# TensorE in written order through the prompt's MLP, with lasting score rows, tanh in PSUM and pair sums moved behind the MLP

## The chip, the core and the metric

The kernel runs on one core of a Trainium2 chip. The metric is device time of one execution in microseconds (us). Engines are named as in the profile: PE (TensorE, matrix products), DVE (VectorE), ACT (ScalarE), POOL (GpSimd) and SP (SyncE, which issues the DMAs). Each engine works through its own queue in a fixed order and waits on semaphores; In this kernel POOL is given operands in SBUF alone.

## The reference

One encoder layer is run on a prompt of 512 rows and, with the same weights, on a sample of 1024 rows, 1024 columns wide, all in float32.

```python
h = _rmsnorm(x, norm_attn_g[l])
z = h @ w_in[l]                         # q | k | v | ca | cb
a_out = _window_attn(q, k, v, bias, band, attn_sink[l])
c = ca * jax.nn.sigmoid(cb)
c = _dwconv(c, conv_dw_w[l], conv_dw_b[l])                     # 31 taps
c = jax.nn.silu(_layernorm(c, conv_ln_g[l], conv_ln_b[l]))
x = x + jnp.concatenate([a_out, c], axis=-1) @ w_out[l]
h = _rmsnorm(x, norm_ffn_g[l])
u = _dwconv(h @ w_up[l], ffn_dw_w[l], ffn_dw_b[l])             # 3 taps
x = x + (jax.nn.silu(u[..., :D_FF]) * u[..., D_FF:]) @ w_down[l]
return _rmsnorm(x, norm_final_g)

# in _window_attn: 8 heads of 64, 2 key heads, blocks of 128 queries against 3 blocks of keys
sc = einsum(qb, kb) * HEAD_DIM ** -0.5 + bias                  # masked to |q-k| <= 128
m = max(max(sc), sink)
p = exp(sc - m)
denom = sum(p) + exp(sink - m)
o = einsum(p / denom, vb)
```

## The kernel before

**Numbers.** A float32 product is made of three products of split operands: each operand is written as a high part (`hi`, type fp32r, a cast by ACT) and the low rest (`lo`, a subtraction), and hi x hi, hi x lo and lo x hi are added in PSUM. Weights are split by `split` (lines 142 and 143: the cast on ACT, the subtraction on POOL), activations where they leave PSUM.

**Buffers.** SBUF is cut into slots by size: 15 of 4096 bytes (`q`), 4 for padded conv rows (`c`), 61 of 2048 bytes (`h`), and small ones. A tile takes the free slot that has been free longest. PSUM has 8 banks: three `a`, two `u`, two `b`, one `c`; the table `use` says which job may take which.

**Stages.** (1) The prompt's 14 chunks of the input projection. (2) The same 14 chunks for the two halves of the sample (`step(i, 1)` and `step(i, 2)`), and beside them, as a side job, the prompt's attention, its conv norms, its output projection (`out_half`) and the transposes of its normalised rows for the MLP (`make_h2`, by `transposed`, line 208). (3) The prompt's MLP: 22 steps `ffn_step(k)`, each with two up projections of 24 products (`proj`, lines 249, 250 and 252), three taps (lines 766 and 762) and a `gate`; beside them, the sample's attention, from step `U0` on. (4) The sample's output projection. (5) The sample's MLP up, in a form with seven block products in place of eight, and then the down projection of the prompt and the sample together, for which sums of blocks of the prompt's gates are wanted (`gb`).

**Side jobs.** A side job is a generator. `proj` calls `tick()` after each six products and once more behind a step; a tick adds `rate` to an account and moves the side job by one `yield` for each whole unit in it. The 31-tap convolutions on DVE (line 292, one operation per tap, the accumulator in PSUM) are paced by the same tick, with the credits `conv` (the prompt's) and `late` (the sample's).

**Attention.** For a unit u (one block of 128 queries and one key head, four heads in it), `scores(u)` makes four score products (line 500), adds bias and finds the row's negated maximum in one DVE operation (line 503), takes Exp on ACT with the row's sum (line 512) and of the sink apart (line 516), adds the two (517), takes the reciprocal (518) and scales the four heads (522 on ACT, 524 on DVE or POOL, by the strings `SCB` for the prompt and `SCD` for the sample). `values(u)` turns the probabilities (four transposes by PE, line 545), splits what it gets into hi (ACT, 547) and lo (DVE, 548), and multiplies with the values (559 with hi, 560 with lo). Unit u+1 has its scores in front of unit u's values.

**What sets the order.** Up to the sample's MLP no order is written by hand: the framework's planner puts all instructions of all engines in order by a simulated timeline. From the sample's MLP on, PE stands in written order (`by_hand`, line 1146).

**The gate.** For gate column j of the prompt, ACT writes tanh into an SBUF tile; DVE multiplies (line 790), DVE or POOL multiplies with the value part (791). Of each pair of gates (j even and odd, called e and t), four differences and sums of halves are made at once (801, 805 and 807 on DVE, 803 on POOL), and seven tiles are stored to DRAM as `gb`.

## Time and profile before

| | |
|---|---|
| median of 3 runs | 1585.31 us (1583.26 to 1587.23) |
| profiled execution | 1580.89 us, its span 1579.1 us |
| mean granted TensorE clock in it | 0.983 |
| busy share of the span | PE 96%, DVE 77%, ACT 51%, POOL 44% |
| DMA | 219.97 MB, mean 139 GB/s |

The page lists the busy time of each engine, the span in 40 slices, the DMA queues, the costliest groups of instructions and what ended the idle time before them. A row of a group reads: line, engine, operation, output and inputs by name, shape, count, then busy time, mean duration in ns, and idle time before with its releaser. A row of the timeline reads: start, duration, engine, line, operation, and in brackets the idle time before it. A matmul's duration is longer than the distance to the next start, since matmuls overlap.

### The profile page before, as it was taken

To read this page: it belongs to the slowest core of one execution; us is meant where nothing else is said; L and a number is where in the kernel's file an instruction comes from. 1 tells how busy PE (TensorE), PEld (TensorE's weight loads), DVE (VectorE), ACT (ScalarE), POOL (GpSimd) and SP (SyncE) were. 2 spreads that over 40 slices of the span, in tenths; PEclk is the share of its full clock that TensorE was granted. 3 is DMA by queue.
4 is the path that set the end of the run, shared out by engine and by line. 5 is a ranking of instruction groups with operands and counts; after the bars stand their busy time and mean duration, and the time that the engine had idled before them with its cause. 6 is when DMAs were issued, how large, how long until landed. Compare 5 with 4: busy or idle time off the path is not lost. (4 is left out here: it accounts for less than half of the span.)

```text
span 1579.1 us, 20219 instructions
## 1 busy us (share of the span) xinstructions
PE 1519.8 (96%) x6843; PEld 1237.4 (78%) x6843; DVE 1211.3 (77%) x1661; ACT 805.3 (51%) x1476; POOL 687.1 (44%) x525
## 2 busy tenths in 40 slices
PE   8999998997998998999999999999999999999997
PEld 6778786886887787878887888888888788888886
DVE  7999865765989999775686787788786945668883
ACT  4635655336676676742455444444544633343354
POOL 6642443235575586751133455555555000003355
PEclk9999998997999999999999999999999999999999
DMA  7583255356443443856221333333332582346644
GB/s 233 155 209 90 81 127 136 108 155 161 147 141 106 137 137 104 240 189 201 94 76 53 109 104 100 100 107 101 100 107 73 191 303 77 121 155 219 216 151 160
DMA packets 222157, 219.97 MB, mean 139 GB/s; under 512 B 12532, under 2 KB 162876, under 8 KB 221925
## 3 DMA queue, kind: packets, MB, share of 16 engines
q1 hardware_dynamic: 222053, 218.67, 44.0%
q8 instruction: 54, 0.88, 0.2%
q14 instruction: 50, 0.41, 0.1%
HBM read 158.97 MB, written 60.70 MB: 139 GB/s over the span
## 5 line engine op out<-in xcount | busy, mean ns | idle before, releaser
L143 POOL TENSOR_TENSOR q<-q,q 128x1024 fp32r<-128x1024 f32 x72 | 176.5, 2456 | 94.4 <-ACT q L142 88.3
L866 DVE TENSOR_TENSOR h<-h,h 128x512 fp32r<-128x512 f32 (+2 forms) x202 | 156.0, 804 | 65.4 <-ACT h L870 25.1
L866 POOL TENSOR_TENSOR q<-q,q 128x512 fp32r<-128x512 f32 x82 | 113.6, 1397 | 160.0 <-ACT q L976 154.5
L1318 PE MATMUL w<-h,h 128*128 128x512 f32 x462 | 181.4, 393 | 0.5 <-DVE q L1108 0.5
L1320 PE MATMUL w<-h,h 128*128 128x512 f32 x462 | 181.7, 393 | 0.0
L1319 PE MATMUL w<-h,h 128*128 128x512 f32 x462 | 181.5, 393 | 0.0
L249 PE MATMUL u<-h,q 128*128 128x512 f32 x400 | 165.2, 414 | 10.7 <-DVE h L762 7.9
L250 PE MATMUL u<-h,q 128*128 128x512 f32 x400 | 162.7, 407 | 0.0
L252 PE MATMUL u<-h,q 128*128 128x512 f32 x384 | 155.0, 404 | 1.2 <-POOL q L143 1.2
L990 PE MATMUL w<-h,q 128*128 128x512 f32 x372 | 147.1, 396 | 1.8 <-ACT h L1070 0.9
L992 PE MATMUL w<-h,q 128*128 128x512 f32 x372 | 145.8, 392 | 0.6 <-POOL q L866 0.6
L292 DVE SCALAR_TENSOR_TENSOR c<-c,cvw,c 128x512 f32<-128x512 f32 x184 | 137.6, 748 | 2.1
L991 PE MATMUL w<-h,q 128*128 128x512 f32 x350 | 137.0, 391 | 0.0
L863 POOL TENSOR_TENSOR q<-q,q 128x1024 f32<-128x1024 f32 x12 | 33.2, 2774 | 236.0 <-DVE q L863 219.6
L870 ACT CAST h<-h 128x512 fp32r<-128x512 f32 x120 | 72.0, 619 | 93.7 <-DVE h L866 41.7
L249 PE MATMUL b<-h,q 128*128 128x512 f32 x256 | 102.7, 401 | 2.5 <-DVE d L322 1.6
L1318 PEld LDWEIGHTS w<-h,h 128*128 128x128 f32 x462 | 86.9, 188 | 20.5 <-ACT h L870 0.9
L249 PEld LDWEIGHTS u<-h,q 128*128 128x128 f32 x400 | 78.3, 196 | 31.1 <-DVE h L762 4.2
L142 ACT CAST q<-q 128x1024 fp32r<-128x1024 f32 x72 | 75.1, 1046 | 53.7 <-DMA q<-in_w_in 16.7
L1319 PEld LDWEIGHTS w<-h,h 128*128 128x128 f32 x462 | 86.8, 188 | 19.7
L1320 PEld LDWEIGHTS w<-h,h 128*128 128x128 f32 x462 | 86.8, 188 | 19.5
L252 PE MATMUL b<-h,q 128*128 128x512 f32 x256 | 101.8, 398 | 0.0
(427 smaller groups left out, 3889.8 us busy)
## 6 DMA issues: line engine op xcount, KB each, us to landing
q<-in_w_up SPq DMA_DIRECT2D x88, 512.0 KB
ga<-q SPq DMA_DIRECT2D x64, 256.0 KB
h<-ga SPq DMA_DIRECT2D x57, 256.0 KB
q<-in_w_in SPq DMA_DIRECT2D x28, 512.0 KB
h<-in_w_down SPq DMA_DIRECT2D x52, 256.0 KB
gb<-h SPq DMA_DIRECT2D x77, 128.0 KB
h<-gb SPq DMA_DIRECT2D x35, 256.0 KB
q<-in_x_sample SPq DMA_DIRECT2D x15, 512.0 KB
```

Of the source, the lines that this page charges most:

```text
L143: (nc.vector if dve else nc.gpsimd).tensor_tensor(lo[:], raw[:], hi[:].bitcast(F32), op=ALU.subtract)
L249: nc.tensor.matmul(out, whi[:, kc, :], hi[:], start=(kc == 0), stop=False)
L250: nc.tensor.matmul(out, whi[:, kc, :], lo[:], start=False, stop=False)
L252: nc.tensor.matmul(out, wlo[:, kc, :], hi[:], start=False, stop=(kc == KC - 1))
L292: nc.vector.scalar_tensor_tensor(acc[:], src(t), w(t), acc[:], op0=ALU.mult, op1=ALU.add)
L866: (eng or nc.vector).tensor_tensor(out, a, b, op=ALU.subtract)
L990: nc.tensor.matmul(out, whi[:, s], hi[:], start=(start and c == 0), stop=False, **go)
L991: nc.tensor.matmul(out, whi[:, s], lo[:], start=False, stop=False, **go)
L992: nc.tensor.matmul(out, wlo[:, s], hi[:], start=False, stop=(stop and c == 3), **go)
L1318: nc.tensor.matmul(out, sh[:, c], th[:], start=(p == 0), stop=False)
L1319: nc.tensor.matmul(out, sh[:, c], tl[:], start=False, stop=False)
L1320: nc.tensor.matmul(out, sl[:, c], th[:], start=False, stop=(p == NPAIR - 1))
```

## The change

The change does these things in the stretch from the sample's projections to the end of the prompt's MLP, and a little behind it:

- PE stands in written order there (`manual_schedule` around stages 2 and 3); the other engines are still put in order by the planner.
- For each head there is a lasting row of scores in SBUF (`score_rows`, two heads in a tile of 4096 bytes, four tiles). Its column 0 holds the negated sink, written by DVE once per attention (`sink_columns`). Exp reads columns 0 to nk and writes a fresh tile, so that its row sum has the sink in it. The Exp of the sink and the add go.
- `gate` writes tanh into a PSUM bank of kind `b`, and stores the whole gate (`gt`). The sums of pairs become side jobs (`pair_sums`) that run behind the MLP, wholly on POOL, on gates that are loaded again. The down projection reads the plain blocks out of `gt`.
- One of four heads of the sample is scaled on ACT in place of DVE (`SCD`).
- The sample's keys and values are loaded ahead of the end of the convs (`load_kv`), and the first up weights in the last chunk of the projections. The sample's attention begins one MLP step later (`U0`), and the rates of the side jobs differ.

```diff
-RA, RB, RBO, RD, RN, RE = 1.2, 0.8, 2.5, 0.78, 0.95, 0.9
+RA, RB, RBO, RD, RN, RE = 1.2, 0.8, 2.5, 0.8, 0.95, 1.4
-CL, CLO, CD = 0.7, 0.7, 0.6
+CL, CLO, CD = 0.6, 1.0, 0.6
-SCB, SCD = "aapa", "vaap"
+SCB, SCD = "aapa", "aaap"
-U0 = 1
+U0 = 2
...
+    def sink_columns():
+        for h in range(0, NH, 2):
+            t = sb.tile([2, NT])
+            for n in range(2):
+                nc.vector.tensor_copy(t[:, n, 0:1], nsink[:, h + n:h + n + 1])
+            score_rows.append(t)
...
-                out=p[:, :nk], in0=sc[:, :nk], in1=bias[h][:, off:off + nk], scale=-1.0,
+                out=row_of(h)[:, 1:1 + nk], in0=sc[:, :nk], in1=bias[h][:, off:off + nk], scale=-1.0,
...
-            nc.scalar.activation(pr[j][:, :nk], pr[j][:, :nk], AF.Exp, scale=-1.0, bias=negm[:, j:j + 1],
-                                 accum_out=den[:, j:j + 1])
-        for j in range(GRP):
-            h = kv * GRP + j
-            nc.scalar.activation(es[:, j:j + 1], sinkb[:, h:h + 1], AF.Exp, bias=negm[:, j:j + 1])
-        nc.vector.tensor_tensor(den[:], den[:], es[:], op=ALU.add)
+            p = sb.tile([1 + 3 * P])
+            nc.scalar.activation(p[:, :1 + nk], row_of(kv * GRP + j)[:, :1 + nk], AF.Exp, scale=-1.0,
+                                 bias=negm[:, j:j + 1], accum_out=den[:, j:j + 1])
+            pr.append(p)
...
     pace.update(rate=RB, conv=CB, late=CL)
+    by_hand = tc.manual_schedule(engines={mybir.EngineType.PE})
+    by_hand.__enter__()
     for i in range(npr, nch):
         want_raw(i + 2)
         want_w(i + 1)
+        if i == nch - 1:
+            for half in range(2):
+                want_up_raw(0, half)
...
     drain(side)
+    load_kv()
     drain(convs)
...
     def gate(j, a, b):
-        t = sb.tile([NT])
-        nc.scalar.activation(t[:], a[:], AF.Tanh, scale=0.5)
-        nc.vector.scalar_tensor_tensor(t[:], t[:], 1.0, a[:], op0=ALU.add, op1=ALU.mult)
-        (nc.vector if j % 4 == VG else nc.gpsimd).tensor_tensor(t[:], t[:], b[:], op=ALU.mult)
...
+        th, t = bank("gate"), sb.tile([NT])
+        nc.scalar.activation(th[:], a[:], AF.Tanh, scale=0.5)
+        if j % 4 == VG:
+            nc.vector.scalar_tensor_tensor(th[:], th[:], 1.0, a[:], op0=ALU.add, op1=ALU.mult)
+            nc.vector.tensor_tensor(t[:], th[:], b[:], op=ALU.mult)
+        else:
+            nc.vector.scalar_tensor_tensor(t[:], th[:], 1.0, a[:], op0=ALU.add, op1=ALU.mult)
+            nc.gpsimd.tensor_tensor(t[:], t[:], b[:], op=ALU.mult)
+        nc.sync.dma_start(gt[j][:], t[:])
+
+    def pair_sums(p):
+        e, o, x, y = (sb.tile([NT]) for _ in range(4))
+        nc.sync.dma_start(e[:], gt[2 * p][:])
+        nc.sync.dma_start(o[:], gt[2 * p + 1][:])
+        yield 0.0
+        yield 0.0
+        gp = nc.gpsimd.tensor_tensor
+        gp(x[:, HR], e[:, HR], o[:, HR], op=ALU.add)
+        gp(x[:, HL], e[:, HL], e[:, HR], op=ALU.subtract)
+        gp(e[:, HR], x[:, HR], e[:, HL], op=ALU.subtract)
+        gp(y[:, HL], o[:, HL], e[:, HR], op=ALU.subtract)
+        for i, src in ((5, x[:, HR]), (7, x[:, HL]), (6, e[:, HR]), (3, y[:, HL])):
+            nc.sync.dma_start(gb[i, p][:], src)
...
         ffn_step(k)
+    by_hand.__exit__(None, None, None)
...
+    side.extend(pair_sums(p) for p in range(NPAIR))
...
-                    nc.sync.dma_start(t[:, 0:n * HT].rearrange("c (q t) -> c q t", t=HT), gb[i, p][:, 0:n, :])
+                    for q in range(n):
+                        j, h = {1: (0, HL), 2: (1, HL), 4: (1, HR)}.get(i, (0, None))
+                        src = gb[i, 2 * p + q][:] if h is None else gt[2 * (2 * p + q) + j][:, h]
+                        nc.sync.dma_start(t[:, q * HT:(q + 1) * HT], src)
```

Three places show the new order. The first is PE at the end of the prompt's output projection. Lines 640 to 642 (before) and 648 to 650 (after) are its products, line 208 are the transposes of the four blocks of scaled rows (the four `q` operands, the last one from the last block), and lines 249 to 252 are projections of the sample's last chunks. Before:

```order
L642 MATMUL u_165_3248<-h_502_3101,h_434_2721 128x512
L208 MATMUL a_166_3307<-ident,q_518_3299 128x128
L208 MATMUL a_166_3307<-ident,q_519_3301 128x128
L208 MATMUL a_167_3316<-ident,q_518_3299 128x128
L208 MATMUL a_167_3316<-ident,q_519_3301 128x128
L249 MATMUL b_168_3325<-h_83_525,q_494_3077 128x512
L250 MATMUL b_168_3325<-h_84_526,q_494_3077 128x512
L208 MATMUL a_166_3307<-ident,q_520_3303 128x128
L208 MATMUL a_167_3316<-ident,q_520_3303 128x128
L252 MATMUL b_168_3325<-h_83_525,q_495_3078 128x512
```

And after:

```order
L650 MATMUL u_165_3215<-h_497_3062,h_427_2673 128x512
L208 MATMUL a_166_3278<-ident,q_515_3270 128x128
L208 MATMUL a_166_3278<-ident,q_516_3272 128x128
L208 MATMUL a_166_3278<-ident,q_517_3274 128x128
L208 MATMUL a_166_3278<-ident,q_518_3276 128x128
L208 MATMUL a_167_3287<-ident,q_515_3270 128x128
L208 MATMUL a_167_3287<-ident,q_516_3272 128x128
L208 MATMUL a_167_3287<-ident,q_517_3274 128x128
L208 MATMUL a_167_3287<-ident,q_518_3276 128x128
L249 MATMUL b_168_3300<-h_83_525,q_489_3038 128x512
```

Before, the fourth block's transposes came 34 projections later; now they are the fourth and the eighth instruction behind the last output product.

The second place is PE in the middle of the prompt's MLP, at one turn of the sample's probabilities (line 545 before, 553 after) and the products with the values (559 and 560 before, 567 and 568 after). Lines 249 to 252 are the up projection. Before:

```order
L545 MATMUL b_285_5452<-ident,h_830_5173 128x128
L545 MATMUL b_285_5452<-ident,h_831_5178 128x128
L545 MATMUL b_285_5452<-ident,h_832_5190 128x128
L545 MATMUL b_285_5452<-ident,h_833_5195 128x128
L249 MATMUL u_281_5396<-h_522_3312,q_847_5295 128x512
L250 MATMUL u_281_5396<-h_523_3313,q_847_5295 128x512
L252 MATMUL u_281_5396<-h_522_3312,q_848_5296 128x512
L249 MATMUL u_281_5396<-h_524_3321,q_847_5295 128x512
L250 MATMUL u_281_5396<-h_525_3322,q_847_5295 128x512
L252 MATMUL u_281_5396<-h_524_3321,q_848_5296 128x512
L249 MATMUL u_281_5396<-h_526_3338,q_847_5295 128x512
L250 MATMUL u_281_5396<-h_527_3339,q_847_5295 128x512
```

And after:

```order
L553 MATMUL a_288_5258<-ident,h_789_4985 128x128
L553 MATMUL a_288_5258<-ident,h_790_4987 128x128
L553 MATMUL a_288_5258<-ident,h_791_4989 128x128
L553 MATMUL a_288_5258<-ident,h_792_4991 128x128
L249 MATMUL u_287_5245<-h_525_3313,q_817_5148 128x512
L250 MATMUL u_287_5245<-h_526_3314,q_817_5148 128x512
L252 MATMUL u_287_5245<-h_525_3313,q_818_5149 128x512
L249 MATMUL u_287_5245<-h_527_3322,q_817_5148 128x512
L250 MATMUL u_287_5245<-h_528_3323,q_817_5148 128x512
L252 MATMUL u_287_5245<-h_527_3322,q_818_5149 128x512
L567 MATMUL b_286_5229<-h_831_5225,h_545_3440 128x512
L568 MATMUL b_286_5229<-h_832_5226,h_545_3440 128x512
```

Before, 24 projections followed the turn shown; now a tick of six does, then the value products of the turn before it, and after one more tick (in some places two) those of the turn itself.

The third place is POOL in the same stage: line 143 writes the low half of an up weight (the first name is its slot). The other lines are the conv's adds (285), gates, scaled heads and sums. Before:

```order
L143 TENSOR_TENSOR q5_768_4792<-q13_745_4653,q10_767_4791 128x1024
L791 TENSOR_TENSOR h2_744_4648<-h2_744_4648,h34_740_4638 128x512
L803 TENSOR_TENSOR h38_770_4799<-h2_744_4648 128x256
L143 TENSOR_TENSOR q9_784_4894<-q2_766_4789,q11_783_4893 128x1024
L524 TENSOR_SCALAR h26_739_4622<-h26_739_4622,s19_734_4596 128x384
L285 TENSOR_TENSOR h46_755_4730<-h46_755_4730,h48_775_4852 128x512
L143 TENSOR_TENSOR q13_794_4960<-q8_772_4811,q4_793_4959 128x1024
```

And after:

```order
L143 TENSOR_TENSOR q9_702_4437<-q0_691_4366,q4_701_4436 128x1024
L579 TENSOR_TENSOR h33_659_4166<-h60_699_4418,h52_698_4417 64x512
L285 TENSOR_TENSOR h46_710_4495<-h46_710_4495,h52_731_4613 128x512
L143 TENSOR_TENSOR q1_720_4532<-q13_695_4378,q0_719_4531 128x1024
L285 TENSOR_TENSOR h46_710_4495<-h46_710_4495,h34_735_4642 128x512
L532 TENSOR_SCALAR h43_709_4482<-h43_709_4482,s3_705_4451 128x384
L807 TENSOR_TENSOR h48_721_4536<-h48_721_4536,h37_717_4525 128x512
L285 TENSOR_TENSOR h46_710_4495<-h46_710_4495,h2_748_4708 128x512
L143 TENSOR_TENSOR q9_730_4602<-q2_718_4529,q13_729_4601 128x1024
```

Before, the low halves went through the slots q5, q9, q13, q2, q8, q3 and q7 in turn; now they alternate between q9 and q1, so each is written where PE has just read the one before the last.

More of the change, by code (lines that the diff above doesn't have):

```diff
@@ L493, in scores @@
         q = qt.pop(u)
[L494 removed]
+        negm, den = sm(GRP), sm(GRP)
         pr = []
@@ L718, in prompt, with want_up_raw @@
         yield from make_h2(0, 0)
+    seq = [(GR[0], j) for j in range(NJ)]
+    upr, upw, pus = {}, {}, {}
+    def want_up_raw(k, half):
+        if k < len(seq):
+            upr[k, half] = chunk_raw(w_up[0], half * FF + seq[k][1] * P)
     side.append(prompt())
     pace.update(rate=RB, conv=CB, late=CL)
+    by_hand = tc.manual_schedule(engines={mybir.EngineType.PE})
+    by_hand.__enter__()
     for i in range(npr, nch):
@@ L817, in ffn_step @@
         gate(k, ug[0], uv[0])
-    use.update(attn="ab")
-    for half in range(2):
-        want_up_raw(0, half)
+    use.update(attn="ab", gate="b")
     for half in range(2):
@@ L1007, in tile_hybrid_encoder @@
         if i == 8:
-            side.append(turned(1, old_bank))
+            side.appendleft(turned(1, old_bank))
         for n in range(2):
```

48 lines of the change are left out of this document (13 added, 35 removed).

## The prediction

> **What bounds the kernel now.** I read the page first (engines, granted clock), then the windows by stage, then TensorE's own waits in each stage, then the groups of VectorE and GpSimd in the stage with most waits, and last the timeline around three places.
>
> ```profile
> PE 1519.8 (96%) x6843; PEld 1237.4 (78%) x6843; DVE 1211.3 (77%) x1661; ACT 805.3 (51%) x1476; POOL 687.1 (44%) x525
> PEclk9999998997999999999999999999999999999999
> 100.00:345.00 245.00, 234.77 (x1080) 191.46 (x1079) 185.12 (x323) 122.11 (x267) 83.51 (x65) 0.98 0.41 115
> 345.00:390.00 45.00, 35.61 (x154) 28.50 (x154) 27.69 (x53) 24.66 (x55) 21.31 (x13) 0.85 0.76 202
> 390.00:680.00 290.00, 272.30 (x1248) 222.15 (x1248) 266.12 (x442) 198.14 (x402) 194.51 (x121) 0.96 0.47 145
> 680.00:820.00 140.00, 140.00 (x671) 115.19 (x670) 92.56 (x132) 54.78 (x105) 42.75 (x53) 1.00 0.42 138
> 820.00:1579.00 759.00, 745.89 (x3260) 606.16 (x3258) 553.10 (x595) 355.76 (x575) 279.34 (x204) 1.00 0.40 134
> ```
>
> After the stretch, its length and TensorE (PE), a windows row gives PEld, DVE, ACT, POOL, then granted clock and DMA. TensorE is the bound; the change adds no matmul, so it can only win back idle time and slow clock, and only in the three stages whose order it changes: the sample's projections with the prompt's attention (100 to 345), the passage into the prompt's MLP (345 to 390), and that MLP with the sample's attention (390 to 680). Idle there: 10.2 + 9.4 + 17.7 = 37.3 us. Slow clock: 245 x 0.02 + 45 x 0.15 + 290 x 0.04 = 4.9 + 6.8 + 11.6 = 23.3 us. So the stages hold 15.1, 16.2 and 29.3 us, 60.6 in all, and no more than that can be won.
>
> The clock follows the idle time:
>
> ```profile
> 531.40 0.55 PE L545 MATMUL b<-ident,h 128*128 128x128 f32 x3 [2.15 <-DVE h L524]
> 533.20:536.60 3.40, 3.40 (x10) 2.68 (x9) 3.40 (x7) 2.56 (x4) 1.64 (x1) 0.50 0.00 0
> 536.60:545.00 8.40, 8.40 (x41) 7.01 (x40) 8.31 (x18) 6.95 (x17) 4.84 (x4) 1.00 0.35 108
> ```
>
> A wait of 2.15 us was followed by 3.4 us at half clock, in which 10 matmuls started where the next stretch's rate gives 16: a stall of 2 to 3 us costs some 1.5 us more. The Trainium skill, "TensorE: Matmul & The Clock Gate", Part 1, says that the throttle returns after at least one idle window of about 3.4 us. By that rule the MLP stage, whose longest wait is 3.4 us, would hardly win clock back, and the time below would be about 9 us higher, 1567; the row shows the loss after 2.15 us, so I count the clock with the stalls.
>
> **Off VectorE in the MLP stage.** Who ends TensorE's waits (window 390 to 680, three largest of seven), and VectorE's groups there:
>
> ```profile
> PE u L249 <- DVE h L762: 6.0, 5, 3.1
> PE a L545 <- DVE h L524: 3.9, 2, 3.4
> PE b L500 <- DVE h L548: 3.2, 3, 1.7
> ...
> L292 DVE SCALAR_TENSOR_TENSOR c<-c,cvw,c 128x512 f32<-128x512 f32 x92 | 68.5, 744 | 0.3
> L790 DVE SCALAR_TENSOR_TENSOR h<-h,h 128x512 f32<-128x512 f32 x19 | 23.8, 1253 | 2.1 <-ACT h L789 2.1
> L517 DVE TENSOR_TENSOR s<-s,s 128x4 f32<-128x4 f32 x15 | 14.0, 931 | 2.0 <-ACT s L516 1.8
> L524 DVE TENSOR_SCALAR h<-h,s 128x384 f32<-128x384 f32 x12 | 12.3, 1024 | 0.1
> L801 DVE TENSOR_TENSOR h<-h,h 128x256 f32<-128x256 f32 x9 | 12.1, 1347 | 0.7 <-POOL h L791 0.6
> L805 DVE TENSOR_TENSOR h<-h,h 128x256 f32<-128x256 f32 x9 | 8.5, 947 | 0.1
> L807 DVE TENSOR_TENSOR h<-h,h 128x256 f32<-128x256 f32 x9 | 6.9, 764 | 0.0
> ```
>
> The three hold 13.1 of the 17.7 us idle, and VectorE, which ends them all, is busy 266 of 290 us. The change takes off it: the sink's add (L517, 14.0), since the sink is now column 0 of a lasting score row that Exp sums itself; the scaling of one head in four (L524, 12.3), now ScalarE's; the three sums of each pair (L801, L805, L807: 27.5). The gate's first product (L790) reads tanh from PSUM; nearest row for one PSUM and one SBUF operand of that width is L292 with 744 ns, so 19 x (1.253 - 0.744) = 9.7. Together 63.5 us: VectorE falls to about 203 of 290, 70%. Between bounds: nothing from L790 (54) to all of these with the waits behind them. On ScalarE some 14 scalings come in (a 512-wide cast there takes 0.57 us, row below: at most 8 us) and the stage's 64 Exp of one column go; it is busy 198 of 290, cost zero. Its cover is gone if ScalarE stands above 90%. The eight copies of one column at the start of each attention cost VectorE at most L517's 0.93 us each, 7.4 us a stage and hidden in the same 30%: zero on the path.
>
> **Written order in the MLP stage.** Here is what can eat the gain. Before, the planner left long stretches of projections between a turn of the probabilities (L545) and the product with the values; now these stand two ticks apart, at the least two times six projections and four transposes. One place shows what must fit:
>
> ```profile
> 153.02 0.39 PE L249 MATMUL b<-h,q 128*128 128x512 f32 x1
> ...
> 155.75 0.39 PE L249 MATMUL b<-h,q 128*128 128x512 f32 x1
> ...
> 504.74 0.60 PE L545 MATMUL a<-ident,h 128*128 128x128 f32 x4
> 507.18 0.57 ACT L547 CAST h<-b 128x512 fp32r<-128x512 f32 x1
> 507.96 2.39 DVE L524 TENSOR_SCALAR h<-h,s 128x384 f32<-128x384 f32 x1
> 510.27 1.51 DVE L805 TENSOR_TENSOR h<-h,h 128x256 f32<-128x256 f32 x1
> 512.36 0.67 DVE L548 TENSOR_TENSOR h<-b,h 128x512 fp32r<-128x512 f32 x1
> 513.09 0.62 PE L500 MATMUL b<-q,h 128*128 128x384 f32 x2 [1.67 <-DVE h L548]
> ```
>
> Twelve projections take 2.73 us (first two rows), so one takes 0.228. From a turn's end to the second value product that needs the low half: 12 x 0.228 + four transposes about 0.4 (of the 0.60 to their end) + one product 0.23 = 3.4 us; where a tick brings nothing, 1.4 more, 4.8. In the rows the turn ended at 505.34 and the low half at 513.03: 7.7 us, too long. But 3.9 us of it are L524 and L805, which leave VectorE; 3.8 remain, of which 1.8 are spent before the cast begins. Cast and subtraction by themselves are 0.57 + 0.67 = 1.3. So the new gap lies between 1.3 (engines free) and 3.8 (this place without the moved work): mostly enough, not always. There are 44 such pairs in the stage. At 0 to 0.6 us each (3.8 + some queue against 3.4 to 4.8) that is 0 to 26 us; I take 0.15, nearer the free end because VectorE has 30% idle, so 6.5 us. Banks and taps (L762, L500 rows above, 9.2 us) I put at 1.5, and 1 of clock. Left over 9 of 29.3: **gain 20**.
>
> A second new wait is in the same stage. The four score rows take four of the 15 large buffers, and the low half of the up weights, which went through seven buffers, now alternates between two. So GpSimd's split can begin only when TensorE has done with the same half one step earlier:
>
> ```profile
> L143 POOL TENSOR_TENSOR q<-q,q 128x1024 fp32r<-128x1024 f32 x36 | 89.4, 2484 | 24.7 <-ACT q L142 23.4 <-issue 1.1
> L803 POOL TENSOR_TENSOR h<-h 128x256 f32<-128x256 f32 x9 | 7.1, 792 | 0.2
> ```
>
> One half lasts 24 x 0.228 = 5.5 us bare; two full splits would not fit, one (2.48) does with 3.0 to spare. Behind the waiting split stand the conv's adds, the gate products and one scaled head; GpSimd is busy 194.5 of 290 and loses L803, so I take zero. It costs if a split starts over 3 us after the half before it.
>
> Tanh in PSUM holds one of the five banks of the attention for a tanh and one product, 0.57 + 0.74 us by the cast's and L292's rows, against the two ticks until that bank comes round again (2.7 us): zero, unless the tanh waits for late taps. The rates move conv steps and side jobs between the stages and leave their number: zero, with VectorE's 24% idle in 100 to 345 as cover for the conv that CLO = 1.0 pulls forward.
>
> **The passage, 345 to 390.** Waits in the window, and the chain of two rows of the prompt from output projection (L645) to the scaled row (L690) that the transposes L208 turn:
>
> ```profile
> PE b L500 <- DMA q<-ksd: 2.5, 2, 1.5
> PE u L249 <- ACT h L210: 1.9, 1, 1.9
> ...
> 339.45 0.68 DVE L645 TENSOR_TENSOR q<-u,q 128x512 f32<-128x512 f32 x1
> 340.17 1.06 ACT L651 ACTIVATE h<-q 128x1024 bf16<-128x1024 f32 x1 [6.68 <-DVE q L645]
> 342.29 0.75 DVE L690 TENSOR_SCALAR q<-q,rs 128x1024 f32<-128x1024 f32 x1
> 345.98 0.68 DVE L645 TENSOR_TENSOR q<-u,q 128x512 f32<-128x512 f32 x1
> 352.69 0.75 DVE L690 TENSOR_SCALAR q<-q,rs 128x1024 f32<-128x1024 f32 x1 [2.20 <-POOL rs L127]
> ```
>
> The keys' loads come before the up weights on SP's queue and the sample's attention one step later (U0 = 2), so the waits for ksd and qsd go. In their place TensorE meets the first turn straight behind the last output product: it waits the whole chain, 3.6 us (339.45 to 343.04) to 7.5 us (345.98 to 353.44, with up-weight work in between). Before, 34 projections covered it. I take 4, since in the new order the up splits stand behind that chain on ScalarE and GpSimd; then 1.5 for three banks against eight turns, 2 of clock, 0.5 for the first up weights, late behind 12 more loads. Left over 8 of 16.2: **gain 8**, between 4 and 12.
>
> **Stage 100 to 345.** Rows of its waits:
>
> ```profile
> PE a L559 <- ACT q L547: 2.2, 1, 2.2
> PE b L353 <- ACT q L350: 0.8, 1, 0.8
> ```
>
> In written order v's transposes (L353) stand right behind their projection: 0.8 to 1.2 us, twice. The four conv norms' second turns come 12 to 18 projections (2.7 to 4.1 us) behind the first with statistics, two GpSimd steps and a scaling between: about 1 each. Twenty value pairs at 0.15: 3. First output product, 12 projections earlier than before, 1.5; clock 2; sum 13 of 15.1: **gain 2**, between -8 and 8.
>
> **Afterwards.** GpSimd gets four sums of each of 11 pairs, 44 x 0.79 = 35 us, in 680 to 820, where it is busy 43 of 140 and no matmul waits; the even and odd gates come back by 22 loads, and the MLP's three plain blocks are now read from them.
>
> ```profile
> gb<-h SPq DMA_DIRECT2D x77, 128.0 KB
> ```
>
> SP has 46 more issues over some 900 us, none in TensorE's waits. The Trainium skill, "GPSIMD Engine Reference", section 8, warns that GpSimd shares SBUF interfaces with VectorE's two-input operations; were all 35 us added to VectorE there, it would be 128 of 140, still no bound. I take a loss of 3 (from -1 to 8) for the planner's new order in this stretch and the last one.
>
> **Sum.** 20 + 8 + 2 - 3 = 27. The profiled execution took 1580.9 (span 1579.1): 1553.9. The median shown is 4.4 above it: 1585.3 - 27 = **1558**. About 0.3% is what a measurement of this kernel can tell from no change.
>
> **Rivals.** (1) Value products come too early, the slower side: the low half takes up to 7.7 us, as in the rows above, against 3.4 to 4.8, so that a pair waits 0.8 us in the mean. 64 pairs x 0.8 = 51, their clock 10, and the other leftovers above (8 + 10 + 2.5) and the 3 of afterwards make 85 against 60.6: 1609 (1590 to 1640). For it: VectorE works in order, with conv steps between. Against: 63 us leave it. It decides from 0.5 us a pair on. (2) The splits' buffers: 40 halves at 0.5 us and a little clock take the MLP's 20 back: 1580 (1572 to 1590). Against it the 3.0 us to spare. (3) Nothing comes of it, gains and new stalls cancel: 1581 to 1590. (4) Written order works as well as from 820 on, where 759 us lose 13: the three stages' 580 us would then lose 10 in place of 60.6, and with the 3 of afterwards it is 1538.
>
> **Chances.** Forecast (1541 to 1571) 0.60, rival 2 as a smaller gain 0.12, rival 4 and beyond 0.06, rival 3 0.08, rival 1 0.14. Faster by over 0.3% (under 1580.5): 0.78; within: 0.08; slower: 0.14. The range 1538 to 1590 leaves out rival 1 and half of rival 4, under 0.2.
>
> **What would show it.** In the stage of the MLP: VectorE about 70%, TensorE's waits below 8 us, hardly any for L548's counterpart, clock 0.99. At the first turn of the prompt's MLP rows one wait of about 4 us for the scaled row and a half-clock stretch behind it. No waits for ksd. GpSimd busier after the MLP, TensorE still at 100%. I am wrong if waits of value products or of the first low-half matmul of a half fill the MLP stage.

## The result and the profile after

| | before | after |
|---|---|---|
| median, us | 1584.28 (1577.65 to 1587.23) | 1605.36 (1600.67 to 1609.69) |
| profiled execution, span, us | 1579.1 | 1604.0 |
| ratio after to before | | 1.0148, interval 1.0126 to 1.0170 |

The change makes the kernel 21 us slower; 1558 was forecast, with a range up to 1590. First the engines from the page of the changed kernel, then its windows by stage (columns as in the prediction, the last stretch cut at 860):

```profile
PE 1523.5 (95%) x6843; PEld 1237.2 (77%) x6843; DVE 1154.1 (72%) x1604; ACT 795.4 (50%) x1396; POOL 709.5 (44%) x558
100.00:345.00 245.00, 213.68 (x939) 170.73 (x938) 170.16 (x300) 106.29 (x217) 73.30 (x57) 0.94 0.37 105
345.00:390.00 45.00, 38.57 (x169) 31.06 (x168) 27.08 (x38) 15.68 (x25) 10.63 (x14) 0.96 0.59 173
390.00:680.00 290.00, 286.37 (x1369) 236.87 (x1368) 221.33 (x426) 211.35 (x399) 195.53 (x119) 0.99 0.46 145
680.00:820.00 140.00, 131.62 (x604) 106.66 (x603) 78.17 (x102) 47.41 (x91) 74.11 (x88) 0.98 0.62 200
820.00:860.00 40.00, 33.04 (x178) 26.71 (x177) 29.13 (x41) 22.30 (x41) 18.60 (x18) 0.91 0.30 94
860.00:1604.00 744.00, 729.22 (x3157) 591.43 (x3155) 541.27 (x578) 342.47 (x551) 271.37 (x199) 1.00 0.41 135
```

The same two stretches of the kernel before, where the prediction's table ran on in one:

```profile
820.00:860.00 40.00, 39.79 (x204) 32.85 (x203) 28.49 (x39) 24.21 (x39) 12.40 (x10) 1.00 0.18 53
860.00:1579.00 719.00, 706.10 (x3058) 573.31 (x3056) 524.61 (x557) 331.56 (x536) 266.94 (x195) 1.00 0.41 138
```

Idle time plus slow clock (length times what the clock lacks to 1), as the prediction reckons a stage's loss:

| stage | before | left over by the prediction | after |
|---|---|---|---|
| 100 to 345 | 15.1 | 13 | 31.3 + 14.7 = 46.0 |
| 345 to 390 | 16.2 | 8 | 6.4 + 1.8 = 8.2 |
| 390 to 680 | 29.3 | 9 | 3.6 + 2.9 = 6.5 |
| 680 to 860 | 0.2 | 3 more in all | 8.4 + 2.8 + 7.0 + 3.6 = 21.8 |
| 860 to the end | 12.9 | | 14.8 |

The two stages on which most of the forecast rested won 8.0 and 22.8 us where 8 and 20 were said. The prompt's MLP runs on behind 680, though: its last tap ends at 717.4 us before and at 724.9 after. From 680 to 720 the changed kernel lost 4.0 + 3.6 = 7.6 us and the kernel before nothing, so through 720 the MLP's gain is 15, less than forecast. The stage with the smallest forecast lost 31 us more than before, and the time from 720 to 860 lost 11.3 + 2.8 = 14.1 us against 0.2. The differences in the table add up to 23.6 of the 24.9 us between the spans; a stretch fixed in time holds slightly other work in a later kernel, so each line is good to a few us.

TensorE's waits in the changed kernel, 100 to 345 us (us in total, times, longest):

```profile
PE a L612 <- DMA q<-cvd: 5.5, 1, 5.5
PE b L249 <- DVE q L361: 5.0, 2, 2.6
PE a L624 <- DVE h L618: 4.9, 2, 4.0
PE a L568 <- DVE q L556: 3.4, 2, 2.4
PE u L512 <- DMA h<-qsd: 2.9, 1, 2.9
PE a L512 <- DVE c L292: 2.4, 1, 2.4
PE u L649 <- DVE q L143: 1.8, 2, 0.9
PE u L649 <- DVE h L143: 1.6, 3, 1.1
PE b L353 <- ACT q L350: 1.4, 2, 0.7
PE u L624 <- DVE h L618: 1.1, 1, 1.1
PE u L612 <- DMA h<-cvd: 0.8, 1, 0.8
```

L612 and L624 are the first and second turn (transposes by TensorE) of a conv norm. The longest waits from 680 to 860 us:

```profile
PE t L928 <- DVE h L881: 4.5, 1, 4.5
PE u L249 <- DVE h L777: 4.0, 1, 4.0
PE c L648 <- ACT h L631: 3.4, 1, 3.4
```

One conv norm of the changed kernel, from its first turn to its second (timeline, TensorE's projections between left out):

```profile
241.70 0.60 PE L612 MATMUL u<-ident,h 128*128 128x128 f32 x4
...
243.28 0.70 DVE L614 BATCH_NORM_STATS2 s<-u 128x6 f32<-128x512 f32 x1
...
244.60 0.17 DVE L615 BATCH_NORM_AGGREGATE s<-s 128x2 f32<-128x6 f32 x1
...
244.85 1.29 POOL L579 TENSOR_TENSOR d<-q,h 64x512 fp32r<-64x512 f32 x1
246.23 2.34 POOL L143 TENSOR_TENSOR q<-q,q 128x1024 fp32r<-128x1024 f32 x1
...
248.65 0.19 POOL L126 TENSOR_SCALAR s<-s 128x1 f32<-128x1 f32 x1
248.93 0.57 POOL L127 TENSOR_TENSOR s<-s,nhalf 128x1 f32<-128x1 f32 x1
...
249.53 0.81 DVE L618 TENSOR_SCALAR h<-u,s,s 128x512 f32<-128x512 f32 x1 [4.76 <-POOL s L127]
...
250.49 1.08 PE L624 MATMUL a<-ident,h 128*128 128x128 f32 x4 [4.03 <-DVE h L618]
```

The statistics are ready at 244.77, but GpSimd's two small steps stand behind a 64x512 operation (L579) and a weight split (3.6 us together). From turn to turn it takes 8.2 us; the written order puts 12 to 18 projections between, 2.7 to 4.1 us. The first turn can meet a queue as well. Here SP issues the load of its input behind four stores of q, and TensorE waits 5.48 us:

```profile
272.36 2.57 SPq L331 DMA_DIRECT2D qsd<-c  x4
275.02 0.57 SPq L606 DMA_DIRECT2D q<-cvd  x1
278.16 1.12 PE L612 MATMUL a<-ident,q 128*128 128x128 f32 x4 [5.48 <-DMA q<-cvd]
```

The place at v (first the transposes in the step bank, then the projection that needs that bank again), and the windows rows behind it:

```profile
168.89 0.66 PE L353 MATMUL b<-ident,q 128*128 128x128 f32 x4 [0.68 <-ACT q L350]
...
172.05 0.42 DVE L361 TENSOR_TENSOR q<-b,q 128x256 fp32r<-128x256 f32 x1
...
172.62 0.77 PE L249 MATMUL b<-h,q 128*128 128x512 f32 x1 [2.36 <-DVE q L361]
172.60:176.00 3.40, 3.38 (x9) 2.82 (x10) 0.00 (x0) 0.23 (x2) 0.00 (x0) 0.50 0.37 136
176.00:180.00 4.00, 4.00 (x17) 3.42 (x16) 1.43 (x5) 2.90 (x8) 1.25 (x1) 0.73 0.00 0
```

The transposes themselves waited 0.68 us, a little less than forecast; the bank that they fill is what the next projection waits for, 2.36 us. Then nine matmuls run at half clock in 3.4 us, and the half clock goes on to about 178 us.

### The profile page after: what moved, and what is told of

Same layout as the page of the kernel before. It is cut to its first block, busy times and chain, and to the rows that moved or that the text cites. A ratio compares the mean times of both kernels' runs of the same rounds, so it can differ in the third digit from the quotient of the medians.

```text
span 1604.0 us, 20129 instructions
## 1 busy us (share of the span) xinstructions
PE 1523.5 (95%) x6843; PEld 1237.2 (77%) x6843; DVE 1154.1 (72%) x1604; ACT 795.4 (50%) x1396; POOL 709.5 (44%) x558
## 5 line engine op out<-in xcount | busy, mean ns | idle before, releaser
L143 POOL TENSOR_TENSOR q<-q,q 128x1024 fp32r<-128x1024 f32 x71 | 171.0, 2412 | 118.6 <-ACT q L142 36.5
L249 PE MATMUL u<-h,q 128*128 128x512 f32 x400 | 163.3, 408 | 4.9 <-DVE h L777 4.0
L250 PE MATMUL u<-h,q 128*128 128x512 f32 x400 | 158.5, 396 | 0.0
L252 PE MATMUL u<-h,q 128*128 128x512 f32 x384 | 151.5, 395 | 1.2 <-POOL q L143 1.2
L249 PE MATMUL b<-h,q 128*128 128x512 f32 x256 | 108.7, 425 | 6.6 <-DVE q L361 5.0
L250 PE MATMUL b<-h,q 128*128 128x512 f32 x256 | 105.0, 410 | 0.0
L1339 PEld LDWEIGHTS w<-h,h 128*128 128x128 f32 x462 | 86.7, 188 | 19.6
L252 PE MATMUL b<-h,q 128*128 128x512 f32 x240 | 98.5, 411 | 0.0
```

What stands on the lines that cost most here:

```text
L143: (nc.vector if dve else nc.gpsimd).tensor_tensor(lo[:], raw[:], hi[:].bitcast(F32), op=ALU.subtract)
L249: nc.tensor.matmul(out, whi[:, kc, :], hi[:], start=(kc == 0), stop=False)
L250: nc.tensor.matmul(out, whi[:, kc, :], lo[:], start=False, stop=False)
L252: nc.tensor.matmul(out, wlo[:, kc, :], hi[:], start=False, stop=(kc == KC - 1))
L1339: nc.tensor.matmul(out, sl[:, c], th[:], start=False, stop=(p == NPAIR - 1))
```

## The experiments

They are numbered e1 to e18 by their labels, and grouped here by what they tell apart. Lines of kernels with before's score code are eight lower than the changed kernel's (L616 for L624 and so on). Ratios are to the kernel before on the same chip.

**Which half of the change costs.** e1 sets written order only from the prompt's MLP on; e2 leaves it out up to the MLP's end.

```diff
 (e1, e2)  side.append(prompt()) ...
-    by_hand = tc.manual_schedule(engines={mybir.EngineType.PE})
-    by_hand.__enter__()
     for i in range(npr, nch):
 (e2 also, behind the MLP's loop)
-    by_hand.__exit__(None, None, None)
 (e1 only, ahead of the MLP's loop)
+    by_hand = tc.manual_schedule(engines={mybir.EngineType.PE})
+    by_hand.__enter__()
     for k in range(NJ):
```

> The changed kernel, but written order begins only with the prompt's MLP; the sample's projections are left to the planner. Theory A (written order is what costs 34 us in the stage 100 to 345): that stage's idle time and slow clock fall from 46 us to some 15, the MLP keeps its gain, time 1570 to 1578. Rival B (the four lasting score rows take buffers and delay loads and splits there, whatever the order): the stage stays above 35 us, time 1597 to 1608.

> The changed kernel without any written order before the sample's MLP; rows, tanh in PSUM, moved sums and early loads stay. Theory A with VectorE's relief as the cause of the MLP's gain: MLP stage loses under 12 us, time 1570 to 1580. Theory A with written order as the cause: MLP stage loses 25 us or more as before the change, time 1588 to 1600.

e1: 1582.8, ratio 1.0004 (0.9986 to 1.0023). e2: 1576.6, ratio 0.9965 (0.9947 to 0.9983). So most of the loss comes with written order ahead of the MLP: without it the changed kernel is 23 us faster. e1 lies between its two theories; its stage 100 to 345 still lost 18.1 + 12.3 = 30 us, so something besides the order is lost there too. e2 came out by its first theory: with no written order at all its MLP stage lost 6.4 + 2.9 = 9.3 us, against 29.3 before and 11.3 in e1. With the rest of the change in place, written order wins nothing in that stage that these two runs show.

**Written order in the MLP without the relief** (the kernel before, with the two lines above ahead of the MLP's loop and their end behind it): rival 1.

> The kernel before, with written order in the prompt's MLP alone and nothing taken off VectorE. If short gaps behind the turns need VectorE's relief (rival 1 of the prediction), value products wait and the MLP stage loses 35 us or more, time 1592 to 1620. If written order alone makes the gain, the stage loses under 15 us, time 1565 to 1578.

1574.1, ratio 0.9941 (0.9924 to 0.9959). The time is that of the second theory, the stage lies between the two: 390 to 680 lost 16.4 + 5.8 = 22 us, 7 less than before. Another 12 were won in the passage (4.0 lost), and 7.6 more were lost from 680 to 860. Value products (L559 and L560) did wait 13 us in the MLP stage, against 3.6 in the changed kernel. So rival 1's mechanism exists without the relief, but at 0.3 us for each of 44 pairs in place of 0.8, and its loss does not come of it.

**The sums at once, as before.** The gate of the kernel before in the changed kernel (tanh in SBUF, no sums after the MLP).

```diff
-    side.extend(pair_sums(p) for p in range(NPAIR))
-        th, t = bank("gate"), sb.tile([NT])
+        t = sb.tile([NT])
+        ... (the sums of a pair in gate, as before)
```

> The changed kernel with the gate as before: tanh in SBUF, the sums of pairs at once and on VectorE, seven tiles stored. If the moved sums cause the 15 to 20 us that the changed kernel loses behind the MLP, that part falls to some 5 and the MLP loses 5 to 20 more, time 1592 to 1612, with no wait over 3 us between 690 and 860. If something else causes them (the later attention, the rates), the waits behind the MLP stay, time 1605 to 1625.

1602.3, ratio 1.0123 (1.0078 to 1.0168), and no wait over 3 us between 690 and 860 us: the first theory. From 720 to 860 it lost 2.7 + 1.4 = 4.1 us in place of 14.1, so some 10 us there come with the moved sums. From 680 to 720 it lost 10.7 in place of 7.6; that part is not the sums'. The MLP stage lost 9.7 in place of 6.5.

**The lasting rows.** e5 puts them alone into the kernel before, e6 takes them alone out of the changed kernel.

```diff
 (e5; e6 is the reverse)
-            p = sb.tile([3 * P])
             nc.vector.tensor_tensor_reduce(
-                out=p[:, :nk], ...
+                out=row_of(h)[:, 1:1 + nk], ...
-            nc.scalar.activation(es[:, j:j + 1], sinkb[:, h:h + 1], AF.Exp, bias=negm[:, j:j + 1])
-        nc.vector.tensor_tensor(den[:], den[:], es[:], op=ALU.add)
```

> The kernel before with the lasting score rows alone (the sink as column 0 of a row, Exp over 1 + nk columns, no separate Exp and add of the sink); everything else is before's, the planner's order too. In the runs with the relief and without written order from 100 to 345 us TensorE still lost about 33 us there against 18 in the kernel before. Theory A: it is the rows, because they change in which order the planner sets the attention against the projections. Then this kernel loses some 12 to 16 us in 100 to 345, wins 3 to 6 in the prompt's MLP (14 us less of VectorE there), and takes 1588 to 1598. Theory B: it is something else of the change (the conv's rates, the loads moved). Then 100 to 345 is as before and the time is 1575 to 1584.

> The changed kernel with before's score buffers and sink (a fresh buffer for each head, four Exp of one column, one add); written order, tanh in PSUM, moved sums and the loads stay. Theory A (rows cost about 15 us in 100 to 345, written order about 18 more): 1584 to 1596, with the wait of 5.5 us for the conv's input at 270 gone or under 2 us. Theory B (in written order the rows don't matter, since the planner no longer sets TensorE's order): 1602 to 1612, with VectorE in the MLP stage at 235 to 245 of 290 us.

e5: 1584.9, ratio 1.0013 (0.9996 to 1.0029). e6: 1607.4, ratio 1.0154 (1.0136 to 1.0172). In e5 the stage 100 to 345 lost 17.3 + 7.4 = 25 us against 15.1, less than theory A had, and the passage won it back (4.5 against 16.2). The MLP stage won nothing (31.1 lost against 29.3), and VectorE was busy 266 us there as before, not 14 less. So where the planner sets the order, rows make the first stage worse. But in written order they matter nothing (theory B): e6 is as slow as the changed kernel. Its VectorE was busy 218.6 us in the MLP stage, not the 235 to 245 expected. Rows are the cause of e1's remainder (e11, which is e1 with old rows, lost 13.5 us in that stage), not of the result.

**Written order of the first stage alone.** e11 is e6 with written order only from the MLP on.

> The changed kernel with before's score buffers and written order only from the prompt's MLP on: against the run with old rows and written order throughout (1607) it takes away the written order in 100 to 390 us alone. Theory A (that written order costs about 30 us there against an order of the planner that before's attention gives): 100 to 345 us loses about 18 to 20 us as in the kernel before, the MLP stage under 10, and the time is 1566 to 1578. Theory B (the loads moved ahead, the rates or U0 cost the stage its time, whoever sets the order): 1583 to 1598.

1581.6, ratio 1.0000 (0.9983 to 1.0017). Windows row of e6, then of e11:

```profile
100.00:345.00 245.00, 212.15 (x947) 173.37 (x946) 168.98 (x305) 112.11 (x250) 72.30 (x53) 0.93 0.37 105
```

```profile
100.00:345.00 245.00, 233.91 (x1075) 189.50 (x1074) 185.08 (x320) 122.64 (x268) 84.00 (x65) 0.99 0.41 115
```

Losses of 50.0 and 13.5 us: the written order of this stage is the cause, and from e6 to e11 the median falls by 26 us, more than the change costs. The time lies between the two theories, 3.6 us above the first: the passage and the MLP lost 9.9 and 14.3 us.

**Which places of the written order.** e9 gives v's transposes another bank, e10 gives the conv norms' input another queue, e14 (on e6 with e9's edit) puts two more ticks between the turns of the prompt's conv norms.

```diff
 (e9, e14)
-            pt = bank("step")
+            pt = bank("step" if g == 0 else "turn")
 (e10)
-        nc.sync.dma_start(cv[:], cvd[...
+        (nc.scalar if G["g"] == 0 else nc.sync).dma_start(cv[:], cvd[...
 (e14)
-        for _ in range(YN):
+        for _ in range(YN + 2 * (G["g"] == 0)):
             yield 0.0
```

> The changed kernel with v's four transposes (sample's two halves) in one of the three banks a instead of one of the two step banks b. In the changed kernel TensorE waited twice 2.5 us at the next projection (169.9 and 183.6 us) for VectorE to empty that step bank, with half clock behind each. Theory A (the held bank is the wait): both waits for L361 go, with 2 to 3 us of clock: 1594 to 1600. Theory B (the wait only moves, to the transposes behind ScalarE's copy or to the attention's banks a): 1602 to 1608.

> The changed kernel with the four loads of the prompt's conv output (cvd, input of the conv norms) issued from ScalarE's queue instead of SP's. In the changed kernel TensorE waited 5.5 us at 272 us for such a load, which stood on SP's queue behind stores of q. Theory A (the queue is the cause): that wait falls under 1 us, with the clock behind it 5 to 8 us: 1596 to 1601. Theory B (the conv's data come late, or ScalarE now waits in SP's place and holds its casts up): 1602 to 1612.

> The kernel with old rows and written order throughout (1607.4) with v's transposes in a bank a (worth 6.7 in the run alone, so 1600 to 1601 without more), and the second turn of the prompt's four conv norms two ticks later, 24 projections behind the first in place of 12. Theory A (in written order the second turn comes before GpSimd's two steps and VectorE's scaling are done; in the run with old rows those waits were 5.0, 6.3 and 5.1 us): those waits fall under 2 us each: 1586 to 1594. Theory B (the time between turns is no matter, since what delays the scaling is work queued ahead of it that moves along): 1597 to 1604.

e9: 1598.7, ratio 1.0106 (1.0083 to 1.0129): 6.7 us won, both waits for L361 gone at the projection (1.1 us came back at a score). e10: 1605.7, ratio 1.0152 (1.0127 to 1.0177): a miss. The wait for cvd fell from 5.5 to 2.9 us, but nothing of it reached the time, and waits for the low halves and for q grew from 3.4 to 4.7 and from 2.9 to 3.8. e14: 1578.2, ratio 0.9971 (0.9952 to 0.9990), 29 us faster than e6. The waits of e6 at the second turns:

```profile
PE u L616 <- DVE q L610: 6.3, 1, 6.3
PE a L616 <- DVE h L610: 5.9, 2, 5.0
PE u L616 <- DVE h L610: 5.1, 1, 5.1
```

and of e14 (the turn is L617 there), with one conv norm of its timeline and the stage's windows row:

```profile
PE a L617 <- DVE q L611: 1.3, 1, 1.3
238.99 0.60 PE L605 MATMUL a<-ident,h 128*128 128x128 f32 x4
...
240.17 2.40 POOL L143 TENSOR_TENSOR q<-q,q 128x1024 fp32r<-128x1024 f32 x1
...
243.53 0.81 DVE L611 TENSOR_SCALAR h<-a,s,s 128x512 f32<-128x512 f32 x1
...
246.29 0.60 PE L617 MATMUL u<-ident,h 128*128 128x128 f32 x4
100.00:345.00 245.00, 228.06 (x1044) 186.02 (x1043) 174.83 (x311) 119.16 (x262) 80.79 (x59) 0.97 0.43 121
```

A weight split stands ahead of the norm's small steps here too, but the turn comes 6.7 us after the first (239.59 to 246.29) and meets its row ready since 244.34. The 17.3 us of waits are 1.3, the stage's clock 0.97 against 0.93. With e9's 6.7 us taken off, if they hold here too, the two ticks are worth 22 us. Theory A's time was even too high by 8. No run has this edit on the changed kernel itself, whose second turns waited 6.0 us in all (4.9 + 1.1) and not 17.3.

**The time after the MLP.** e7 leaves the sums' four operations out and keeps their loads and stores; e8 and e13 change the pace of side work.

```diff
 (e7)
-        gp(x[:, HR], e[:, HR], o[:, HR], op=ALU.add)
-        ... (the other three)
 (e8, e13)
-... RE = ... 1.4
+... RE = ... 0.9      (e13: 2.0)
```

> The changed kernel without the four GpSimd operations of each pair's sums after the prompt's MLP: the loads and the four stores of a pair stay (what is stored is not the sums). It tells the 35 us of GpSimd from the transfers. Theory A (GpSimd's sums delay the norms' and conv's steps that TensorE waits for between 690 and 860): 1592 to 1598, waits above 3 us at 740 to 840 gone. Theory B (the transfers or the pace of side work delay them, or the order of the planner): 1602 to 1609, with the same waits.

> The changed kernel with RE, the pace of side work after the prompt's MLP, at 0.9 as before instead of 1.4. Theory A (side work pulled forward too fast is what TensorE meets unready between 690 and 860): 1592 to 1599. Theory B (the pace is no cause): 1602 to 1609, with waits of the same size.

> The changed kernel with RE, the pace of side work after the prompt's MLP, at 2.0 instead of 1.4 (0.9 gave 1618). 48 ticks at 1.4 call for about 67 pieces of side work, against 44 of the pair sums, 30 of six conv norms and 5 of the turned rows; what is left over is drained in one lump ahead of the last rows. Theory A (that lump of sums is what TensorE meets at 820 to 840, and at 0.9 the larger lump of 13.8 us): with 2.0 nothing is left over, the wait of 4.5 us at 831 and its half clock go: 1594 to 1601. Theory B (the sums cost the same wherever they stand): 1602 to 1609.

e7: 1595.9, ratio 1.0073 (1.0057 to 1.0089): the arithmetic of the sums costs 9.4 us by the medians. That is theory A's time but not all of its picture, since a wait of 3.9 us appeared at a conv norm's second turn (773 us). From 720 to 860 it lost 5.9 + 1.4 = 7.3 us; from 680 to 720 it lost 7.7 as in the changed kernel. e8: 1618.0, ratio 1.0214 (1.0198 to 1.0230), slower than both theories: at the low pace most sums are left for the lump ahead of the last rows. TensorE's longest wait there was 13.7 us. e13: 1606.3, ratio 1.0136 (1.0113 to 1.0159): theory B. At 2.0 the wait for the turned rows shrinks (4.5 to 1.4 us), and that for the conv norm's last cast grows from 3.4 to 6.1.

**Sums on VectorE, and none moved.**

```diff
 (e12 on e11; e17 on e14, with RE = 2.0)
-        gp = nc.gpsimd.tensor_tensor
+        gp = nc.vector.tensor_tensor
 (e18 on e14: the gate of the kernel before, as e4)
```

> The kernel of the run before (old rows, written order only from the prompt's MLP on) with the four sums of a pair after the MLP on VectorE instead of GpSimd. Theory A (the sums hurt because GpSimd's queue holds the two steps of each norm's and each row's scaling factor behind them): 5 to 9 us faster than the run before. Theory B (any 35 us of work there delay the chain, on VectorE as on GpSimd, or VectorE's queue is the tighter one): same within 3 us, or slower.

> The run e14 (written order throughout, old rows, v's turn in a bank a, second turns of the conv norms two ticks later: 1578.2) with the pair sums on VectorE and RE at 2.0. At RE 2.0 the wait of 4.5 us ahead of the last rows went in both runs that tried it, but a wait for the output projection's input (conv norm's last cast) grew to 5 to 6 us, with the norm's two GpSimd steps queued among the sums. Theory A (with the sums off GpSimd that wait shrinks too): 1566 to 1573, the fastest run. Theory B (the norms' chain is late for another reason, the pace or VectorE's own queue): 1575 to 1582.

> The run e14 with the gate of the kernel before (tanh in SBUF, a pair's sums at once on VectorE, nothing of them after the MLP). Theory A (moving the sums only shifts the loss): the 390 to 680 stage loses some 8 to 12 us more, 690 to 860 some 9 to 10 less, and the time stays within 1573 to 1582. Theory B (with written order repaired VectorE's load in the MLP is what counts): 1583 to 1592.

e12: 1579.1, ratio 0.9979 (0.9964 to 0.9993), 2.5 us under e11: theory B by its bound, GpSimd's queue is at most a small part. The wait for the turned rows was 6.9 us there, 4.5 in e11. e17: 1572.9, ratio 0.9910 (0.9887 to 0.9932); e18: 1573.9, ratio 0.9918 (0.9898 to 0.9938). Both times lie in theory A's range, and both are 4 to 5 us faster than e14 by the medians. They cannot be told from e3 (1574.1), which takes the kernel before and sets written order in the MLP alone. In e17 the wait for the last cast did not shrink (3.4 + 2.7 us against 2.9 + 0.5 in e14), so theory A's reason is not shown. e18's windows rows of the MLP and of what follows:

```profile
390.00:680.00 290.00, 276.17 (x1291) 224.95 (x1291) 234.34 (x436) 212.24 (x450) 196.52 (x122) 0.98 0.46 142
680.00:860.00 180.00, 178.48 (x864) 146.24 (x863) 120.58 (x169) 79.71 (x144) 56.29 (x65) 1.00 0.37 122
```

19.6 us lost in the MLP, 1.5 behind it. In e17 it was 6.6 and 15.1. So moving the sums moves the loss: in e14, with the sums moved, 8.2 and 14.2 us were lost in these two stretches. What of it, beside the 9.4 us of arithmetic, is their 22 loads and 44 stores and what the side work's order, was not told apart.

**Rows for the sample alone.** Before's buffers in the prompt's attention, rows in the sample's, the rest as e11; then with RE at 2.0.

```diff
 (e15 on e11)
+        old = G["g"] == 0
...
-            p = sb.tile([3 * P])
+            if old:
+                pr.append(sb.tile([3 * P]))
```

> Written order only from the prompt's MLP on, tanh in PSUM and moved sums as in the change, before's score buffers for the prompt's attention, lasting rows for the sample's alone. Theory A (rows cost by the planner's order of the prompt's attention only, and save VectorE's sink add in the MLP stage): 100 to 345 us as before (18 to 20 lost), MLP stage under 6 us lost: 1568 to 1576. Theory B (the rows gain nothing in the MLP stage): 1578 to 1584, as the run with old rows in both (1581.6).

> The run before (rows for the sample only, written order from the prompt's MLP on) with RE at 2.0. By theory A of the pace it is 5 to 8 us faster than that run, 1560 to 1570, and the fastest so far; by theory B the same within 3 us.

e15: 1579.5, ratio 0.9958 (0.9939 to 0.9976). e16: 1576.6, ratio 0.9955 (0.9941 to 0.9969). e15's stage 100 to 345 lost 13.9 us, like the kernel before, as theory A said. But its time is theory B's: the MLP stage lost 11.3 in place of under 6, only 3 less than e11. Pace 2.0 brings nothing clear of the noise here either.

## Why the prediction was wrong, point by point

**The step that failed: "Stage 100 to 345".** Its sum was 13 us left over; measured are 46.0. By its terms, from the waits of the changed kernel above:

| term | forecast | measured |
|---|---|---|
| v's transposes | 2 | 1.4 |
| the bank that they hold (L249 behind L361) | not listed | 5.0 |
| first turns of the conv norms (load of cvd) | not listed | 6.3 |
| second turns | 4 | 6.0 |
| value pairs | 3 | 3.9 |
| first scores (q's load, VectorE) | not listed | 5.3 |
| first output products | 1.5 | 3.4 |
| clock | 2 | 14.7 |

Three waits were put at nothing without a reason, 16.6 us together; with the clock they are most of what is missing. e1, and e11 against e6, show that the written order of the stage is what loses the time. Which wait is worth how much is measured for the bank alone: 5.0 us of waits, 6.7 with its clock (e9). For the load, another queue brought no time (e10).

**The second turns** were put at "about 1 each" for "statistics, two GpSimd steps and a scaling". That counts the steps bare (0.70 + 0.17 + 0.19 + 0.57 + 0.81 = 2.4 us in the rows above) and leaves out what stands ahead of them on GpSimd, 3.6 us in the row shown. The prediction asked of the up splits what is queued behind them, and did not ask it here. In the changed kernel it cost only 2 us more than forecast, which is luck: one of the four turns waited 4.0 us, the others 1.1, 0.9 and nothing. In e6, the same order with old rows, it was 17.3 us of waits, and 22 us of time by e14. Why the rows shift the waits from the one place to the other is open, and no run moved the two steps out of GpSimd's queue.

**The clock** was put at 2 and is 14.7. The prediction's price, some 1.5 us of half clock to a wait of 2 to 3 us, met too few waits and was itself too low. The stage has seven waits over 2 us. Half clock stood beside and behind six of them, three times for 3.4 us (waits of 2.9, 2.4 and 4.0 us) and three times for 6.8 (2.4, 2.6 and 5.5 us), 15.4 us lost in all by windows of 0.5 us; the seventh, 2.4 us at 265, had none (clock 1.00 from 262 to 268). What the Trainium skill, "TensorE: Matmul & The Clock Gate", Part 1, says of an idle window of about 3.4 us does not fit the row at 172.60: the wait was 2.36 us.

**"Afterwards".** 35 us of sums were laid beside GpSimd's 97 idle us and called nearly free (3). Their arithmetic costs 9.4 us by e7, and 720 to 860 lost 14.1 us against 0.2. Why is open: GpSimd's two steps of each norm stand in the same queue, but with the sums on VectorE (e12) the kernel was only 2.5 us faster.

**Right in mechanism, near in size.** The MLP from 390 to 680: its value products wait 1.8 + 1.0 + 0.8 = 3.6 us where 6.5 was forecast, no wait for a low half of the up weights, clock 0.99. Behind 680 the window of the forecast missed 7.6 us of the same MLP. The gain was forecast for relief and written order together; e2, the change without written order, has most of it (9.3 lost against 29.3). The relief was smaller than summed: VectorE 221 us against 203. One term of it was hardly there. The sink's add was put at 14.0 us, but e6, which keeps the add, has VectorE at 218.6 us:

```profile
L517 DVE TENSOR_TENSOR s<-s,s 128x4 f32<-128x4 f32 x16 | 5.0, 313 | 7.9 <-ACT s L516 7.9
```

Tanh in PSUM did a little more than its term; the row of the changed kernel's groups beside L790's 1253 ns:

```profile
L806 DVE SCALAR_TENSOR_TENSOR h<-b,h 128x512 f32<-128x512 f32 x15 | 10.3, 685 | 2.7 <-ACT b L801 2.6
```

The passage: the wait for the scaled row 3.4 us (4 forecast), for the three banks 3.1 (1.5), clock 1.8 (2).

**The rivals.** The time lies near rival 1's 1609, but not for its reason: value pairs were to wait 51 us, and in the two stages they waited 3.9 + 3.6. Even without the relief (e3) it was 13 us in the MLP stage. What rivals 2 and 3 took away in the MLP was not lost either. A loss in the stage with the smallest forecast had no rival of its own.

## What to carry to other kernels

When an order is written out, list every pair of dependent TensorE steps, and for each pair the whole queue in front of each helper step between them, not the helper's own durations; the distance in projections must cover that. A load's place in its queue and a bank that a step holds count like a step. In e14 two ticks more between two turns were worth some 22 us, as much as the whole gain of the MLP stage. And idle share on an engine does not make added work free: 35 us of sums beside 97 idle us cost 9. It pays to try the parts apart: e3, written order in the MLP alone, was 9 us faster than the kernel before, while the whole change was 21 us slower.

## What the runs showed of the hardware

The same 256-wide sums took very different times by where they run. In the MLP of the kernel before, on VectorE beside a busy GpSimd, L801 took 1347 ns, L805 947 and L807 764 (rows in the prediction). Afterwards on VectorE in e12, with GpSimd busy 35 of the 140 us from 680 to 820, and on GpSimd in the changed kernel, where they were moved:

```profile
L807 DVE TENSOR_TENSOR h<-h,h 128x256 f32<-128x256 f32 x11 | 4.6, 421 | 15.8 <-DMA h<-gt 15.8
L818 POOL TENSOR_TENSOR h<-h,h 128x256 f32<-128x256 f32 x11 | 9.7, 883 | 10.8 <-DMA h<-gt 10.1 <-DVE d L630 0.6
```

Those means hide two kinds. Of the 27 sums of the kernel before in that stage, the 12 that no GpSimd operation overlapped took 0.41 or 0.42 us, and the nine that took over 1 us all lay beside GpSimd operations. The sink's add, of four columns, shows it best. At 597.70, with GpSimd idle, it took 0.14 us; here it ended with the second of two GpSimd operations:

```profile
524.78 1.28 POOL L571 TENSOR_TENSOR h<-h,h 64x512 fp32r<-64x512 f32 x1
524.92 3.52 DVE L517 TENSOR_TENSOR s<-s,s 128x4 f32<-128x4 f32 x1
526.03 2.40 POOL L143 TENSOR_TENSOR q<-q,q 128x1024 fp32r<-128x1024 f32 x1
```

So a mean such as L517's 931 ns is not the add's own work but mostly time held beside GpSimd, and it can vanish when the neighbours move, as in e6. With one operand in PSUM the gate's first product took 0.68 or 0.69 us in all 15 cases of the changed kernel's stage, also where GpSimd ran beside it all the time; with both operands in SBUF, in the kernel before, 0.67 to 3.16. The Trainium skill, "GPSIMD Engine Reference", section 8, names VectorE's operations with two SBUF inputs as those that contend with GpSimd; the trace agrees, 0.14 us against 3.52 for the same add.
